# Block sums made beside the second half's input, and a norm between the layers without empty places, in a two-layer trunk

## The chip, the cores and the metric

The kernel runs on one core of one Trainium2 chip. The metric is the device time of one execution in microseconds (us); the median of three runs of the kernel before is 2228.72 us (2227.24 to 2230.06).

## The reference, cut to what matters

Two layers (DEPTH = 2) over x of 1024 positions by 1024 channels, all float32. Per layer, with shift, scale and gate from the conditioning vector:

```python
u = x * (1.0 + scale) + shift
proj = u @ w_in            # a_in, a_gate, b_in, b_gate, q_lat, kv_lat, k_rope, c_gate, merge
# branch A: GLU, causal conv(31), LayerNorm, swish, gate; branch B: short conv, gate
# branch C: latent attention from rms_norm(q_lat), rms_norm(kv_lat), k_rope
m = g_a * y_a + g_b * y_b + g_c * y_c
x = layer_norm(ALPHA * x + gate * (m @ w_o))
```

## The kernel before, in words

**Layout and products.** Everything is stored with channels on the 128 partitions. The 1024 positions are two halves of 512 (T); a tile of u is 128 channels by 512 positions, kept as a pair (high, low) of rounded float32: `split` (L125 to L133) lets ACT round the value (L129) and DVE subtract it for the remainder (L130). Each product block is three matmuls (high·high, high·low, low·high: L186 to L188 in `chunk`, L295 in `pair_jobs`).

**u and its sums.** The eight channel tiles of half h are `state["u", l, h]`. The same tiles are, by parity of the channel tile, the blocks X11 and X12 (first half), X21 and X22 (second half). `pair_jobs` makes two 128-wide outputs for both halves with seven block products instead of eight; its inputs are X11, X12, X22 and the sums S1 to S4 of four tiles each. `s_job` (L493) makes one tile of each sum: it loads the four x tiles again (`affine`, L456, L459), applies scale and shift on ACT (L462), forms S3 = X11 − X21, S1 = X21 + X22, S2 = X22 − S3, S4 = X12 − S2 on DVE (L498, L501, L503, L506) and splits each into its home (`factor`). Temporary tiles have the tag `w`, six buffers in all, which latents, gates and merge tiles use as well; tag `n` has five.

**Start of a layer.** `build` (L1191 on) makes a list of jobs. For each layer it first writes the latents of the first half (`head(l, 0)`: two chunks of kv, three of q, the kv norm and k_rope; 27 jobs, `lat0`), with a side list woven between them: in layer 0 the eight `u_jobs` of the second half (load, affine on ACT, split into X21 or X22), in layer 1 the norm between the layers, `ln_jobs(0, 1)`. Then come the latents of the second half (`lat1`, 24 jobs), with the four `s_job`s woven between them, then the logit pairs (`lgps`, L860), blended with the up-projections (`kps` and others), and the rest.

**The norm between the layers.** `center_jobs` (L740) has a mean (L757), eight centerings with their squares (L762 to L768), `rstd_jobs` (fold of the squares on PE L530, root and Newton step L534 to L539, a row L515, spread on PE L545) and then `apply` for each of eight tiles: multiplication (L1103, DVE), u of the next layer by ACT straight from it (L1107, `through` holds the combined scale and shift), x itself (L1109), its write to HBM from POOL's queue (L1116), and after each odd tile the two splits into X21 and X22 (`add_u`). X21's tiles take the buffers c0 to c3, which held the residual tiles that are written out. The first half of x was normalized before, within layer 0's last part, and its u tiles are made from HBM by `u_jobs(1, 0)`.

**Order.** The place in the job list sets the priority of an instruction; the queue of each engine is then ordered ahead of the run from these priorities and from which operands and buffers are free, so an instruction can stand in its queue before one of an earlier job. `weave(main, side, start, end)` (L66) spreads the side list evenly over the places start to end of the main list. An empty job (`pause`) takes a place and issues nothing. Weights are loaded up to four units ahead (LOOKAHEAD) on SP's queue, as are the x tiles (L459) and the rope tables.

Of the kernel before, what the change touches and what calls it, by code (L numbers as in the profile page):

```python
# [16 lines left out]
P = 128  # L17
T = 512
# [47 lines left out]
def weave(main, side, start, end):  # L66

    out = list(main[:start])
    n, m, k = end - start, len(side), 0
    for i in range(start, end):  # L70
        out.append(main[i])
        upto = (i - start + 1) * m // n
        out += side[k:upto]
        k = upto
    return out + side[k:] + list(main[end:])
# [25 lines left out]
class Trunk:  # L101
# [388 lines left out]
            nc.vector.tensor_tensor(gb[:, 8:16], gb[:, 8:16], a[:, 1], op=ALU.add)  # L490
        return self.state["through"]

    def s_job(self, l, i):  # L493

        nc = self.nc
        tt = nc.vector.tensor_tensor
        x11, x21 = (self.affine(l, h, 2 * i, act=True) for h in range(2))
        tt(x11, x11, x21, op=ALU.subtract)  # L498
        self.factor(l, "S3", x11)
        x22 = self.affine(l, 1, 2 * i + 1, act=True)  # L500
        tt(x21, x21, x22, op=ALU.add)  # L501
        self.factor(l, "S1", x21)
        tt(x22, x22, x11, op=ALU.subtract)  # L503
        self.factor(l, "S2", x22)
        x12 = self.affine(l, 0, 2 * i + 1, act=True)
        tt(x12, x12, x22, op=ALU.subtract)  # L506
        self.factor(l, "S4", x12)
# [229 lines left out]
            return ([], fn)  # L737
        return [step(k) for k in range(31)]

    def center_jobs(self, tiles, n, st, tags, tot=None):  # L740

        nc = self.nc

        def total(_):
            ts = st["ts"] = tiles()
            if tot is not None:
                st["tot"] = tot()
                return
            st["tot"] = self.t2("n", "tot")
            nc.vector.tensor_tensor(st["tot"], ts[0], ts[1], op=ALU.add)  # L750
            for t in ts[2:]:
                nc.vector.tensor_tensor(st["tot"], st["tot"], t, op=ALU.add)

        def mean(_):
            c = st["ts"][0].shape[-1]
            st["ps"] = self.bank("meanps", tags[0])[:, :c]
            nc.tensor.matmul(st["ps"], self.ones, st["tot"], start=True, stop=True)  # L757

        def center(i):
            def fn(_):  # L760
                t = st["ts"][i]
                nc.vector.scalar_tensor_tensor(t, st["ps"], -1.0 / n, t, op0=ALU.mult, op1=ALU.add)  # L762
                sq = self.t2("n", "lsq", t.shape[-1])
                nc.scalar.activation(sq, t, AF.Square)
                if i == 0:
                    st["ss"] = sq
                else:
                    nc.vector.tensor_tensor(st["ss"], st["ss"], sq, op=ALU.add)  # L768
            return ([], fn)
        pause = ([], lambda _: None)  # L770
        fold, spread = self.rstd_jobs(st, n, "ln", tags[1:])
        return [([], total), pause, ([], mean)] + [center(i) for i in range(n // P)] + [pause, pause, fold, pause, pause, pause, spread]

    def lna_jobs(self, l, h):
# [316 lines left out]
        return self.chunk([(self.wo[l, e, :, 0:T], tags[0]), (self.wo[l, e, :, T:2 * T], tags[1])],  # L1091
                          lambda: self.state["m", l, h], post, "ops", "pj", cols, kept)

    def ln_jobs(self, l, h, cols=slice(0, T)):
        nc = self.nc
        st = {}
        n = cols.stop - cols.start

        def apply(e):
            def fn(_):  # L1100
                r = st["ts"][e]
                v = self.vec[l]
                nc.vector.tensor_tensor(r, r, st["r"], op=ALU.mult)  # L1103
                if l < L - 1 and h == 1:
                    t = self.t2("w", "xu")
                    gb = self.through(l)
                    nc.scalar.activation(t, r, AF.Identity, bias=gb[:, 8 + e:9 + e], scale=gb[:, e:e + 1])  # L1107
                    st["t", e] = t
                nc.scalar.activation(r, r, AF.Identity, bias=v[:, V_LB + e:V_LB + e + 1],  # L1109
                                     scale=v[:, V_LG + e:V_LG + e + 1])  # L1110
                if l == L - 1:
                    dst = self.out[e * P:(e + 1) * P, h * T + cols.start:h * T + cols.stop]
                else:
                    dst = self.pd.tile([P, T], F32, name=f"xD{h}{e}")
                    self.state["x", h, e] = dst
                (nc.sync if l == L - 1 else nc.gpsimd).dma_start(dst, r)  # L1116
                if l < L - 1 and h == 1 and e % 2:

                    for k in (e - 1, e):
                        self.add_u(l + 1, h, k, st["t", k])  # L1120
            return ([], fn)
        return self.center_jobs(lambda: [self.state["r", l, h, e][:, cols] for e in range(8)], 1024, st,
                                ("tp", "tp", "av"), lambda: self.state["rt", l, h, cols.start]) \
            + [apply(e) for e in range(8)]

    def end_jobs(self, l, h, cols):
# [64 lines left out]
    def build(self):  # L1191
        self.setup_early()
        jobs, first, adas = [], [], []
        for l in range(L):
# [3 lines left out]
            if l == 0:  # L1198
                lat0, up0 = self.head(l, 0, (("pj", "pj"), ("pj", "sd", "sd")))
                units = [u for us, _ in lat0[:20] for u in us][:10]  # L1200
                for n in range(4):
                    steps = self.ada_jobs(0, n, early=True)
                    for _, fn in steps[:-1]:
                        fn(None)
                    if n == 0:
                        self.nc.sync.dma_start(self.vec[0], self.vecs[0])
                    steps[-1][1](None)
                    if n == 0:
                        self.setup()
                    for k in range(SP[n], SP[n + 1]):  # L1210
                        first.append(self.load_w((units[k], HOMES["first"][k])))
                    self.u_job(0, 0, 2 * n)
                    self.u_job(0, 0, 2 * n + 1)
                tabs = self.table_jobs()
                part0 = weave(lat0, tabs, 2, len(lat0) - 2)
                side0 = self.u_jobs(l, 1)
                adas = [j for n in range(4, 6) for j in self.ada_jobs(0, n)]
            else:
                lat0, up0 = self.head(l, 0)
                part0 = lat0  # L1220
                side0 = self.ln_jobs(l - 1, 1)
            jobs += weave(part0, side0, 0, len(part0))

            lat1, kvn1, ukv1, qn1, uq1 = self.head(l, 1)
            sums = [([], lambda _, l=l, i=i: self.s_job(l, i)) for i in range(4)]
            jobs += weave(lat1, sums, 3, len(lat1) - 2)

            lg = [self.logit_pair(l, n, 2 * i) for n in range(3) for i in range(4)]
            body = blend(lg[0] + lg[1] + lg[2], up0[:-1] + kvn1 + up0[-1:])
# [32 lines left out]
            else:  # L1262

                kept = [{} for _ in range(8)]
                tags = HOMES["wo"]
# [126 lines left out]
```

## Time and profile before

| | |
|---|---|
| median of 3 runs | 2228.72 us |
| the profiled execution | 2231.88 us, its span 2230.0 us |
| mean granted clock of PE | 0.979 |
| busy: PE, DVE, ACT, POOL | 96%, 81%, 51%, 11% of the span |
| HBM read, written | 254.16 MB, 80.54 MB |

The span is what the profiler saw from the first to the last instruction; the execution's own time is 1.9 us longer. A matmul's end is modelled, so busy PE is not PE at its peak; times between starts of matmuls are the better measure. "Granted clock" is the share of full speed that the throttle gave TensorE: its levels are 1.2 and 2.4 GHz. A line of a timeline gives start, duration, engine, source line, operation, out<-in, shape and count; in brackets stands the idle time of the engine before it and what ended it. L129 and L130 are one line for all splits, so they are told apart by their tiles (`u`, `wsplit`, `latn`).

### The profile page before, as it was taken

The numbers are of one execution on the slowest core, as the hardware profiler recorded it, in microseconds if no ns is written. First come the engines' busy times: TensorE is split into PE (matmuls) and PEld (weight loads), VectorE is DVE, ScalarE is ACT, GpSimd is POOL, SyncE is SP. The second block draws the span as 40 slices with busy tenths as digits, with TensorE's granted clock in tenths as the row PEclk, the third lists the DMA queues.
The fourth block names the chain that finished last, engine by engine and source line by source line (L and its number), as shares of the span: only waits on it lengthen the run. The fifth ranks groups of instructions, "written<-read, shape, count | busy, mean of one in ns | idle before, by whom it ended". The sixth has DMA issues, their size and how long they took to land.

```text
span 2230.0 us, 29769 instructions
## 1 busy us (share of the span) xinstructions
PE 2136.2 (96%) x10097; PEld 1730.9 (78%) x10097; DVE 1809.0 (81%) x2910; ACT 1135.0 (51%) x2072; POOL 235.0 (11%) x483
## 2 busy tenths in 40 slices
PE   8889999999999989998997899999999999999996
PEld 7667778888778778877876688888887778888786
DVE  4676899989997678788868769898898967877886
ACT  2764443333344666666448544443434437666843
POOL 4010100000001331111001101000000023221000
PEclk9999999999999999998999999999999999999998
DMA  7566652332222996766535756432222159746542
GB/s 268 177 187 210 162 186 98 104 104 95 76 81 91 229 240 183 198 175 209 189 111 184 204 164 185 148 109 86 90 81 74 61 156 232 213 128 173 167 148 65
DMA packets 185192, 336.68 MB, mean 151 GB/s; under 512 B 22608, under 2 KB 47440, under 8 KB 185040
## 3 DMA queue, kind: packets, MB, share of 16 engines
q1 hardware_dynamic: 124560, 218.50, 31.6%
q0 software_dynamic: 46656, 91.12, 15.6%
q10 hardware_dynamic: 13824, 25.17, 3.1%
q8 instruction: 79, 1.29, 0.2%
q14 instruction: 73, 0.60, 0.1%
HBM read 254.16 MB, written 80.54 MB: 150 GB/s over the span
## 4 chain that ended last, share of the span: by engine, by line
PE 76%; issue 14%; DMA 4%; DVE 3%; ACT 2%; POOL 1%; SPq 0%; POOLq 0%; DVEq 0%; ACTq 0%
PE lgps L295 18%; PE bgps L295 7%; PE xgps L295 7%; PE aps L295 7%; PE cgps L295 4%; PE agps L295 3%; PE yps L186 3%; PE avps L954 3%; PE yps L187 3%; PE yps L188 3%; PE tps L938 3%; PE ops L186 2%; PE ops L187 2%; PE ops L188 2%; PE score L914 2%
## 5 line engine op out<-in xcount | busy, mean ns | idle before, releaser
L295 PE MATMUL lgps<-u,wsplit 128*128 128x512 f32 x2016 | 485.6, 398 | 14.7 <-ACT lgps L260 12.1
L129 ACT CAST wsplit<-wraw 128x512 fp32r<-128x512 f32 (+1 forms) x524 | 318.5, 615 | 294.1 <-PE yps L188 63.9
L295 PEld LDWEIGHTS lgps<-u,wsplit 128*128 128x128 f32 x2016 | 381.0, 189 | 109.9 <-ACT lgps L260 13.9
L130 DVE TENSOR_TENSOR wsplit<-wraw,wsplit 128x512 fp32r<-128x512 f32 (+1 forms) x524 | 353.1, 678 | 72.0 <-ACT wsplit L129 70.7
L736 DVE SCALAR_TENSOR_TENSOR cacc<-abuf,vec,cacc 128x1024 f32<-128x1024 f32 x240 | 306.5, 1277 | 0.6
L295 PE MATMUL xgps<-u,wsplit 128*128 128x512 f32 x672 | 160.4, 397 | 0.0
L295 PE MATMUL bgps<-u,wsplit 128*128 128x512 f32 x672 | 160.0, 397 | 0.0
L295 PE MATMUL aps<-u,wsplit 128*128 128x512 f32 x672 | 158.1, 395 | 0.0
L295 PEld LDWEIGHTS xgps<-u,wsplit 128*128 128x128 f32 x672 | 126.0, 188 | 31.6 <-issue 1.4
L295 PEld LDWEIGHTS bgps<-u,wsplit 128*128 128x128 f32 x672 | 126.0, 188 | 31.5 <-issue 1.4
L295 PEld LDWEIGHTS aps<-u,wsplit 128*128 128x128 f32 x672 | 126.3, 188 | 30.5
L130 DVE TENSOR_TENSOR pt<-tps,pt 128x512 fp32r<-128x512 f32 (+1 forms) x160 | 98.9, 631 | 26.8 <-ACT pt L129 25.3
L919 DVE TENSOR_REDUCE nm<-score 128x1 f32<-128x384 f32 (+7 forms) x128 | 95.7, 750 | 27.5 <-PE score L917 26.5
L186 PE MATMUL ops<-m,wsplit 128*128 128x512 f32 (+1 forms) x320 | 116.0, 364 | 0.6 <-ACT m L129 0.6
L921 ACT ACTIVATE prob<-score,nm 128x384 f32<-128x384 f32 (+7 forms) x128 | 94.3, 739 | 43.8 <-DVE nm L919 23.4
L186 PE MATMUL yps<-y,wsplit 128*128 128x512 f32 x256 | 111.6, 436 | 4.8 <-ACT y L132 4.2
L954 PE MATMUL avps<-pt,Vh 128*128 128x256 f32 x640 | 110.9, 297 | 3.2 <-ACT pt L129 2.1
L187 PE MATMUL ops<-m,wsplit 128*128 128x512 f32 (+1 forms) x320 | 112.3, 351 | 0.6 <-DVE m L130 0.6
L188 PE MATMUL ops<-m,wsplit 128*128 128x512 f32 (+1 forms) x320 | 112.1, 351 | 0.0
L129 ACT CAST pt<-tps 128x512 fp32r<-128x512 f32 (+1 forms) x160 | 84.0, 540 | 42.7 <-PE tps L938 40.1
L187 PE MATMUL yps<-y,wsplit 128*128 128x512 f32 x256 | 104.0, 406 | 0.2 <-DVE y L133 0.2
L129 ACT CAST wsplit<-wt 128x512 fp32r<-128x512 f32 x112 | 69.5, 620 | 68.0 <-DVE wt L220 47.8
(322 smaller groups left out, 4265.4 us busy)
## 6 DMA issues: line engine op xcount, KB each, us to landing
wraw<-in_win SPq DMA_DIRECT2D x264, 256.0 KB, 2.7
wraw<-in_wout SPq DMA_DIRECT2D x96, 256.0 KB, 3.0
mt<-tD SPq DMA_DIRECT2D x96, 256.0 KB, 4.3
adaraw<-in_wada SPq DMA_DIRECT2D x64, 256.0 KB, 3.5
wraw<-in_wo SPq DMA_DIRECT2D x64, 256.0 KB, 3.2
tD<-mt ACTq DMA_DIRECT2D x48, 256.0 KB, 2.1
Kh<-knD POOLq DMA_DIRECT2D x48, 256.0 KB, 4.6
Vh<-vD POOLq DMA_DIRECT2D x48, 256.0 KB, 5.2
```

Source lines behind the costliest of these rows:

```text
L129: nc.scalar.copy(dst[:, 0], src)
L130: nc.vector.tensor_tensor(dst[:, 1], src, dst[:, 0].bitcast(F32), op=ALU.subtract)
L186: mm(ps, w[:, 0, c], x[k][:, 0, cols], start=k == 0, stop=False)
L187: mm(ps, w[:, 0, c], x[k][:, 1, cols], start=False, stop=False)
L188: mm(ps, w[:, 1, c], x[k][:, 0, cols], start=False, stop=k == n - 1)
L295: mm(ps, w[:, a, c], x[:, e], start=n < 2 and k == 0 and i == 0, stop=k == 3 and i == 2, skip_group_check=True)
L736: nc.vector.scalar_tensor_tensor(acc, a[:, k:k + S], w, acc, op0=ALU.mult, op1=ALU.add)
L914: mm(o, q[0:96, 0, qc], k[0:96, 0, :w], start=True, stop=False)
L919: nc.vector.tensor_reduce(nm[:, 0:1], sp[:, :nk], axis=AX.X, op=ALU.max, negate=True)
L921: nc.scalar.activation(p[:, :nk], sp[:, :nk], AF.Exp, bias=nm[:, 0:1], accum_out=nm[:, 1:2])
L938: nc.tensor.transpose(tp[:, c:c + P], st["p", hd, 2 * half + b][:, (2 * kp + k) * P:(2 * kp + k + 1) * P], self.ident)
L954: mm(av[:, half * 256:(half + 1) * 256], v[:, 2 * kp + k], pt[:, w, (1 - k) * 256:(2 - k) * 256], start=kp == 0 and k == 0 and w == 0, sto ...
```

## The change

`s_job` becomes `su_job`. It is handed the two finished tiles of u of the second half, splits them into X21 and X22 and goes on with the sums of the same four tiles, so that it loads and scales only the two tiles of the first half. In layer 0 four such jobs take the place of the eight `u_jobs`, in layer 1 `apply` calls one after each odd tile. The sums woven into `lat1` go; `lat1` stands alone. In the norm between the layers (`tight`) four of six empty places go (the one after `total`, both before `fold`, one of the three behind it): `total, mean, center x8, fold, pause, pause, spread` instead of `total, pause, mean, center x8, pause, pause, fold, pause, pause, pause, spread`.

```diff
--- before.py
+++ after.py
@@ -490,14 +490,14 @@
             nc.vector.tensor_tensor(gb[:, 8:16], gb[:, 8:16], a[:, 1], op=ALU.add)
         return self.state["through"]
 
-    def s_job(self, l, i):
-
-        nc = self.nc
-        tt = nc.vector.tensor_tensor
-        x11, x21 = (self.affine(l, h, 2 * i, act=True) for h in range(2))
+    def su_job(self, l, i, x21, x22):
+
+        tt = self.nc.vector.tensor_tensor
+        self.add_u(l, 1, 2 * i, x21)
+        self.add_u(l, 1, 2 * i + 1, x22)
+        x11 = self.affine(l, 0, 2 * i, act=True)
         tt(x11, x11, x21, op=ALU.subtract)
         self.factor(l, "S3", x11)
-        x22 = self.affine(l, 1, 2 * i + 1, act=True)
         tt(x21, x21, x22, op=ALU.add)
         self.factor(l, "S1", x21)
         tt(x22, x22, x11, op=ALU.subtract)
@@ -737,7 +737,7 @@
             return ([], fn)
         return [step(k) for k in range(31)]
 
-    def center_jobs(self, tiles, n, st, tags, tot=None):
+    def center_jobs(self, tiles, n, st, tags, tot=None, tight=False):
 
         nc = self.nc
 
@@ -769,6 +769,8 @@
             return ([], fn)
         pause = ([], lambda _: None)
         fold, spread = self.rstd_jobs(st, n, "ln", tags[1:])
+        if tight:
+            return [([], total), ([], mean)] + [center(i) for i in range(n // P)] + [fold, pause, pause, spread]
         return [([], total), pause, ([], mean)] + [center(i) for i in range(n // P)] + [pause, pause, fold, pause, pause, pause, spread]
 
     def lna_jobs(self, l, h):
@@ -1091,7 +1093,7 @@
         return self.chunk([(self.wo[l, e, :, 0:T], tags[0]), (self.wo[l, e, :, T:2 * T], tags[1])],
                           lambda: self.state["m", l, h], post, "ops", "pj", cols, kept)
 
-    def ln_jobs(self, l, h, cols=slice(0, T)):
+    def ln_jobs(self, l, h, cols=slice(0, T), tight=False):
         nc = self.nc
         st = {}
         n = cols.stop - cols.start
@@ -1116,11 +1118,10 @@
                 (nc.sync if l == L - 1 else nc.gpsimd).dma_start(dst, r)
                 if l < L - 1 and h == 1 and e % 2:
 
-                    for k in (e - 1, e):
-                        self.add_u(l + 1, h, k, st["t", k])
+                    self.su_job(l + 1, e // 2, st["t", e - 1], st["t", e])
             return ([], fn)
         return self.center_jobs(lambda: [self.state["r", l, h, e][:, cols] for e in range(8)], 1024, st,
-                                ("tp", "tp", "av"), lambda: self.state["rt", l, h, cols.start]) \
+                                ("tp", "tp", "av"), lambda: self.state["rt", l, h, cols.start], tight) \
             + [apply(e) for e in range(8)]
 
     def end_jobs(self, l, h, cols):
@@ -1213,17 +1214,17 @@
                     self.u_job(0, 0, 2 * n + 1)
                 tabs = self.table_jobs()
                 part0 = weave(lat0, tabs, 2, len(lat0) - 2)
-                side0 = self.u_jobs(l, 1)
+                side0 = [([], lambda _, i=i: self.su_job(0, i, *(self.affine(0, 1, 2 * i + e, act=True) for e in range(2))))
+                         for i in range(4)]
                 adas = [j for n in range(4, 6) for j in self.ada_jobs(0, n)]
             else:
                 lat0, up0 = self.head(l, 0)
                 part0 = lat0
-                side0 = self.ln_jobs(l - 1, 1)
+                side0 = self.ln_jobs(l - 1, 1, tight=True)
             jobs += weave(part0, side0, 0, len(part0))
 
             lat1, kvn1, ukv1, qn1, uq1 = self.head(l, 1)
-            sums = [([], lambda _, l=l, i=i: self.s_job(l, i)) for i in range(4)]
-            jobs += weave(lat1, sums, 3, len(lat1) - 2)
+            jobs += lat1
 
             lg = [self.logit_pair(l, n, 2 * i) for n in range(3) for i in range(4)]
             body = blend(lg[0] + lg[1] + lg[2], up0[:-1] + kvn1 + up0[-1:])
```

## Rows read from the trace of the kernel before

**Rows 1.** The page, its span and the busy time of each engine.

```profile
span 2230.0 us, 29769 instructions
PE 2136.2 (96%) x10097; PEld 1730.9 (78%) x10097; DVE 1809.0 (81%) x2910; ACT 1135.0 (51%) x2072; POOL 235.0 (11%) x483
```

**Rows 2.** Timeline of PE: matmuls behind its longest waits around both layers' starts.

```profile
98.05 0.77 PE L186 MATMUL latps<-u,wsplit 128*128 128x512 f32 x1 [4.10 <-DVE kra L599]
...
131.94 2.93 PE L295 MATMUL lgps<-u,wsplit 128*128 128x512 f32 x6 [5.25 <-ACT lgps L260]
...
1183.18 0.80 PE L186 MATMUL latps<-u,wsplit 128*128 128x512 f32 x1 [7.39 <-ACT u L129]
...
1225.91 0.50 PE L307 MATMUL kps<-latn,wsplit 128*128 128x512 f32 x1 [3.99 <-ACT sq L560]
...
1233.29 2.92 PE L295 MATMUL lgps<-u,wsplit 128*128 128x512 f32 x6 [4.55 <-ACT lgps L260]
```

**Rows 3.** Windows of all engines, around the first latents of layer 0 and of layer 1.

```profile
core 0: us, PE busy (x) PEld busy (x) DVE busy (x) ACT busy (x) POOL busy (x), PEclk, DMA share, GB/s
64.00:98.00 34.00, 28.13 (x127) 20.71 (x127) 25.02 (x48) 28.12 (x50) 2.75 (x5) 0.98 0.56 177
98.00:136.00 38.00, 32.71 (x132) 25.18 (x133) 34.72 (x61) 29.73 (x52) 2.15 (x4) 0.86 0.58 192
1175.00:1198.00 23.00, 15.61 (x61) 11.19 (x60) 17.63 (x32) 18.77 (x31) 4.85 (x9) 0.78 0.39 142
1198.00:1237.00 39.00, 30.45 (x132) 22.98 (x131) 34.44 (x60) 32.73 (x57) 3.23 (x6) 0.87 0.62 200
```

**Rows 4.** Timeline of ACT: the two copies L260 and what stood before each.

```profile
130.79 0.62 ACT L129 CAST u<-xu 128x512 fp32r<-128x512 f32 x1
131.31 0.58 ACT L260 COPY lgps<-lgps 128x512 f32<-128x512 f32 x1
...
1232.13 0.62 ACT L129 CAST u<-xu 128x512 fp32r<-128x512 f32 x1
1232.65 0.58 ACT L260 COPY lgps<-lgps 128x512 f32<-128x512 f32 x1
```

**Rows 5.** Timeline of PE, DVE, ACT: the norm before layer 1, to the last X2 tile.

```profile
1163.98 0.42 PE L530 MATMUL qv<-lsq,ones 128*32 128x128 f32 x8
...
1174.70 0.39 PE L545 MATMUL rstd<-rsrow,onesr 128*128 128x512 f32 x1
...
1175.63 4.26 DVE L1103 TENSOR_TENSOR r<-r,rstd 128x512 f32<-128x512 f32 x7
...
1182.53 1.12 ACT L129 CAST u<-xu 128x512 fp32r<-128x512 f32 x2
...
1195.14 0.62 ACT L129 CAST u<-xu 128x512 fp32r<-128x512 f32 x1 [1.53 <-DMA xD<-r]
```

**Rows 6.** Timeline of ACT: several of one kind in a row.

```profile
1208.35 1.65 ACT L129 CAST u<-xu 128x512 fp32r<-128x512 f32 x3
...
1212.66 2.24 ACT L462 ACTIVATE xu<-xu,ada 128x512 f32<-128x512 f32 x3
```

**Rows 7.** Timeline of DVE: the first subtraction of the first and last job of sums.

```profile
1206.55 0.69 DVE L498 TENSOR_TENSOR xu<-xu 128x512 f32<-128x512 f32 x1 [2.23 <-ACT xu L462]
...
1230.16 0.68 DVE L498 TENSOR_TENSOR xu<-xu 128x512 f32<-128x512 f32 x1
```

**Rows 8.** Waits of SP's queue, 60 to 140 us: in total, times, longest.

```profile
SPq L459 <- DVE u L130: 11.8, 8, 4.5
```

**Rows 9.** Timeline of PE: matmuls at low and at full clock, behind the wait at 98.

```profile
103.30 0.62 PE L186 MATMUL latps<-u,wsplit 128*128 128x512 f32 x1
103.73 0.43 PE L187 MATMUL latps<-u,wsplit 128*128 128x512 f32 x1
103.99 0.39 PE L188 MATMUL latps<-u,wsplit 128*128 128x512 f32 x1
104.22 0.39 PE L186 MATMUL latps<-u,wsplit 128*128 128x512 f32 x1
```

## The prediction

> **What bounds the kernel now.** I read the page first: PE is busy for 2136.2 of 2230.0 us [rows 1]. So at most some 94 us of waiting can be won in the whole span, and only where PE waits in the stretches that the change touches.
>
> The second view is PE's own timeline over the two starts (layer 0 up to 140 us, layer 1 from 1140 us). Five waits of about 4 us or more stand there, 25.3 us together [rows 2]; the reader should look at what each ended on. 7.39 us in layer 1 is the first latent product of the second half, waiting for the first X2 tile. 4.10 us in layer 0 is the same product waiting for a PSUM bank that k_rope's DVE work (L599) had not given back. The other three stand behind the latents: two `lgps` products (5.25 and 4.55 us) end on the copy L260, one `kps` product (3.99 us) on the square L560. L260 and L560 are short ACT instructions that were merely late.
>
> The third view, the windows, says why they were late. While the jobs of sums run (98 to 136 and 1198 to 1237 us) DVE is busy 34.7 of 38 and 34.4 of 39 us, ACT 29.7 of 38 and 32.7 of 39 [rows 3]. In the stretches just before (64 to 98, 1175 to 1198) DVE has 9.0 and 5.4 us to spare, ACT 5.9 and 4.2. ACT's timeline shows both late copies directly behind a cast of a `u` tile [rows 4]; at that place it belongs to a sum. So PE waits for two vector engines that are filled with sums, and just before that they have some room.
>
> The fourth view follows the norm between the layers: squares folded on PE at 1163.98, spread at 1174.70, first multiplication of `apply` at 1175.63, first X21 cast at 1182.53, last X2 cast at 1195.14 [rows 5]. DVE runs seven L1103 in a row, though the code writes them pair by pair: the place in the job list is a priority, not the place in the queue.
>
> **The change, part by part.** *Loads and affines removed.* Per layer the sums no longer load the second half's eight x tiles again: 8 DMAs of 256 KB and 8 affines L462. The loads are worth nothing by themselves: the DMA share in these stretches is 0.39 to 0.62 [rows 3]. The affines cost ACT (2.24 us for three, so 0.75) 6.0 us per layer [rows 6], already left out of the next price.
>
> *Sums moved in front of the second half's latents.* One pair's sums now cost ACT two affines (1.5) and four casts (1.65 us for three, so 0.55 each, 2.2): 3.7 us [rows 6]; DVE eight instructions at 4.26/7 = 0.61 [rows 5]: 4.9 us. They have priority over the next pair's X2 tiles, and PE needs all eight X2 tiles for the first latent chunk. Three pairs' sums lie before the last X2 tile, so it comes later by at most 3 × 3.7 = 11.1 us if ACT sets the pace. It is less where loads and affines of the first half, which wait for nothing of the second, run in ACT's spare time: with all six early, 3 × 2.2 = 6.6 us. It is more if a pair's sums take the pace they have today: 1206.55 to 1230.16 for three jobs is 7.9 us each [rows 7], less two affines 6.4, and 3 × 6.4 = 19.2 us. I take 9.6: one pair's affines early (1.5 us off), the rest in line, because ACT's spare time holds about that and the price of single instructions is nearer to a queue that is never empty. DVE, with 4.9 us a pair against 9.0 and 5.4 to spare, follows within these ends.
>
> *SP and POOL.* On SP the loads of the first half's x (eight a layer) now stand ahead of weights. A load whose buffer is still in use blocks SP: 11.8 us in eight times today [rows 8]. Weights are asked for four units ahead, which covers a few us; with that cover gone it belongs to the upper end, 19.2. POOL's writes of x keep number and order. The first sum of a pair (S1) gains a wait: it overwrites x21, so it follows X21's split, whose cast waits for the write of the residual out of the same buffer (1.53 us before the last cast [rows 5]); behind it on ACT stand only casts of the same pair, counted above.
>
> *What the late sums gave back.* After the latents nothing of the sums is left in front of L260 and L560, so these waits go: 3.99 + 4.55 us in layer 1, 5.25 in layer 0 [rows 2]. Each left a low clock. Behind the 4.10 us wait the matmuls start 0.43 us apart, back to 0.23 from 103.99 on [rows 9]: 13 matmuls took 103.73 − 98.05 = 5.7 us where 13 × 0.23 = 3.0 would do, 2.7 us lost at the low level (1.2 GHz). Behind the two `lgps` waits six matmuls took 2.92 us instead of 1.4 [rows 2], so 1.5 to 2.7 us; I take 2. Behind 3.99 the first matmul ran 0.50 us, near full, so 0 to 2.7: I take 1. Gain: layer 1 3.99 + 1 + 4.55 + 2 = 11.5, layer 0 5.25 + 2 = 7.3 us. Next in line then are the weights' splits, which PE reaches one unit at a time.
>
> In layer 0 the 4.10 us wait with its 2.7 lies inside the latents, where PE will now wait for X2 tiles anyway: 6.8 us of the delay is absorbed there.
>
> *The norm without pauses.* Four of six empty places go and 22 jobs instead of 26 are spread over 27: the mean comes after the third instead of the fourth product job, the fold after the 14th instead of the 15th, the spread after the 18th instead of the 19th. A place is six matmuls of 0.23, 1.4 us. An empty place waits for nothing, so bounds are nothing (the DVE chain, not the place, rules) and half the 10.7 us between fold and spread [rows 5], 5.3; a loss only if PE reached the spread before its row was there, one place, 1.4. I take a gain of one place, 1.4.
>
> *Sum.* Layer 1: −1.4 + 9.6 − 11.5 = −3.3. Layer 0: 9.6 − 6.8 − 7.3 = −4.5. Together −7.8 us. The profiled execution took 2231.9 us around its span of 2230.0; it would take 2224.1. It stands 3.2 us above the median of 2228.7, which becomes 2220.9: 2221.
>
> **The rivals.** *More: the vector engines' spare time takes the sums.* Where all affines of the first half run early, the delay is 6.6 us: layer 0 is 6.6 − 6.6 − 7.3 = −7.3, layer 1 with the norm's best −5.3 + 6.6 − 11.5 = −10.2; together −17.5, 2211. For it: DVE's 9.0 and 5.4 us to spare. Against it: ACT has little more than 4 us just before.
>
> *Slower: the six `w` buffers pace the pairs.* A pair now holds four of them (x21, x22, x11, x12) until S4, and in layer 0 the two kv latents hold two more up to their norm, so one pair at a time gets through. Then today's pace of sums holds, 19.2 us: layer 1 −1.4 + 19.2 − 11.5 = +6.3, layer 0 19.2 − 6.8 − 7.3 = +5.1; +11.4, 2240. For it: 11.8 us of SP's waits on exactly that release [rows 8]. Against it: the chunks' drains shared those buffers and both engines then. It decides from where both layers' delays exceed 11.5 + 14.1 + 1.4 = 27.0, so 13.5 us each, 4.5 a pair.
>
> *No change: the clock takes it back.* X2 pairs come 12.6/3 = 4.2 us apart today [rows 5]; with 3.2 us of sums each it is 7.4, and for each pair PE has 12 matmuls on two banks, 2.8 us at 0.23: waits of over 4 us, as long as those that left a low level above. Then each layer runs a low stretch more, 2.7 each [rows 9]: −7.8 + 5.4 = −2.4, 2226. The Trainium skill, "TensorE: Matmul & The Clock Gate", section on HAM oscillation, speaks against the change in the same way: groups of matmuls shorter than the wait between them begin at the low clock each time. By that rule the sum would be −2.4 instead of −7.8; the trace agrees so far as every wait above 4 us is followed by 0.43 us matmuls, but while the next pair is still missing a slow group costs nothing, and only the last one counts.
>
> **How the numbers follow.** A measurement of this kernel tells about 0.2%, 4.5 us, from no change: faster is below 2224.3, slower above 2233.2. Chances: forecast 0.42 (its own range 2214 to 2227), more 0.20 (2200 to 2215), clock 0.16 (2223 to 2230), slower 0.22 (2231 to 2248). Faster: three quarters of the first, all of the second, a fifth of the third: 0.55. Same: a quarter of the first, most of the third, a tenth of the fourth: 0.25. Slower 0.20. The range 2207 to 2239 leaves out about a third of "more" and half of "slower", under 0.2.
>
> **What would show it.** Right: 16 L462 fewer (eight per layer); the last X2 cast of layer 1 near 1204 instead of 1195; PE's waits on L260 and L560 behind the latents gone, and new, shorter ones on `u` casts between the latent products; DVE fuller in 1175 to 1198. The norm is right if fold and spread come 1 to 2 us earlier. Wrong: waits on L260 as long as before (then it was not the sums), pairs more than 8.5 us apart (slower), or 0.43 us matmuls after each pair up to the last latent (clock).

## The result and the profile after

The change made the kernel slower: 2243.28 us (median of 7 runs, 2235.21 to 2248.02) against 2228.94 us of the kernel before on the same chip, ratio 1.0063, 95% interval 1.0048 to 1.0077, so 10.7 to 17.2 us. The prediction was 2221 us, faster. The profiled execution of after took 2248.02 us, its span is 2246.1.

The page of after, span and busy times:

```profile
span 2246.1 us, 29725 instructions
PE 2140.1 (95%) x10097; PEld 1729.3 (77%) x10097; DVE 1811.3 (81%) x2910; ACT 1124.9 (50%) x2056; POOL 234.8 (10%) x483
```

Against [rows 1] 16 ACT instructions are gone, as the change says. PE is busy 3.9 us longer for the same 10097 matmuls and idle some 12 us longer. Lines of the listing from L771 to L1118 stand two further down in after.

To see where, I cut the start of each layer at three marks that every kernel has. In layer 0 the first is **S**, a matmul of the first half's latents that ends a wait of 0.49 us on a split weight, so that what happened ahead of it drops out; then come the last latent product of the second half and the first product `aps` (the first of the pair products behind the latents). In layer 1 they are the last `prime` (its start), the last latent product and the last `aps`. From before, the timeline of PE (first line) and groups of a tile on PE, which give count, min/median/max ns, and first to last start:

```profile
64.38 0.50 PE L188 MATMUL latps<-u,wsplit 128*128 128x512 f32 x1 [0.49 <-DVE wsplit L130]
L188 PE MATMUL latps<-u,wsplit x59: 387/396/632, 59.9 to 117.8; 128*128 128x512 f32 x59
L295 PE MATMUL aps<-u,wsplit x672: 393/394/399, 217.4 to 1595.8; 128*128 128x512 f32 x168
L203 PE MATMUL prime<-onesr x6: 392/564/793, 1.3 to 1141.3; 128*128 128x512 f32 x6
L188 PE MATMUL latps<-u,wsplit x80: 390/394/796, 1142.0 to 1215.0; 128*128 128x512 f32 x80
```

The same of after:

```profile
62.41 0.50 PE L188 MATMUL latps<-u,wsplit 128*128 128x512 f32 x1 [0.49 <-DVE wsplit L130]
L188 PE MATMUL latps<-u,wsplit x57: 387/397/628, 60.2 to 134.5; 128*128 128x512 f32 x57
L295 PE MATMUL aps<-u,wsplit x672: 393/394/398, 226.5 to 1609.1; 128*128 128x512 f32 x168
L203 PE MATMUL prime<-onesr x6: 392/562/796, 1.3 to 1152.6; 128*128 128x512 f32 x6
L188 PE MATMUL latps<-u,wsplit x80: 391/396/628, 1153.3 to 1237.8; 128*128 128x512 f32 x80
```

**A** (S to the last latent product, layer 0) went from 53.4 to 72.1 us; **B** (from there to the first `aps`) from 99.6 to 92.0; **C** (`prime` to the last latent product, layer 1) from 73.7 to 85.2; **D** (from there to the last `aps`) from 380.8 to 371.3. So both layers lose up to the last latent and get back behind it: layer 1 most of it, layer 0 two fifths. The rest of the run has the same jobs in both, but it is not equally long in every profile: from the first `aps` to `prime` it took 919.5 to 926.1 us over all kernels of this document. So what single profiles add up to A to D is not the difference of the medians to the microsecond.

PE's waits in after, timeline of PE, in answer to [rows 2]:

```profile
83.38 0.73 PE L186 MATMUL latps<-u,wsplit 128*128 128x512 f32 x2 [2.40 <-ACT u L129]
...
97.58 0.80 PE L186 MATMUL latps<-u,wsplit 128*128 128x512 f32 x1 [7.74 <-ACT u L129]
104.91 0.73 PE L186 MATMUL latps<-u,wsplit 128*128 128x512 f32 x2 [1.56 <-ACT u L129]
...
115.19 0.79 PE L186 MATMUL latps<-u,wsplit 128*128 128x512 f32 x1 [4.50 <-ACT sq L560]
...
147.07 6.47 PE L295 MATMUL lgps<-u,wsplit 128*128 128x512 f32 x20 [1.87 <-ACT lgps L260]
...
1194.54 0.79 PE L186 MATMUL latps<-u,wsplit 128*128 128x512 f32 x1 [7.41 <-ACT u L129]
1199.85 0.80 PE L186 MATMUL latps<-u,wsplit 128*128 128x512 f32 x1 [2.00 <-ACT sq L560]
1211.40 0.50 PE L186 MATMUL latps<-u,wsplit 128*128 128x512 f32 x1 [4.12 <-ACT u L129]
...
1250.31 4.93 PE L295 MATMUL lgps<-u,wsplit 128*128 128x512 f32 x20 [1.87 <-ACT lgps L260]
```

What went as foreseen: the L260 waits fell from 5.25 and 4.55 to 1.87 each, and the `kps` wait on L560 is gone. What was not: the 4.10 us of [rows 2] in layer 0 has a successor of 4.50 us on a square, ahead of the same product, and the waits for X2 tiles came on top of it.

Windows of all engines in after: the stretches of [rows 3], then A, then C:

```profile
core 0: us, PE busy (x) PEld busy (x) DVE busy (x) ACT busy (x) POOL busy (x), PEclk, DMA share, GB/s
64.00:98.00 34.00, 21.42 (x91) 14.86 (x89) 24.66 (x43) 25.29 (x43) 1.67 (x3) 0.87 0.56 177
98.00:136.00 38.00, 31.44 (x118) 22.57 (x118) 30.88 (x58) 23.54 (x44) 2.84 (x6) 0.80 0.37 119
62.00:134.50 72.50, 52.96 (x206) 37.57 (x207) 55.60 (x100) 49.41 (x86) 4.37 (x8) 0.84 0.46 147
1152.60:1237.80 85.20, 70.37 (x294) 52.05 (x293) 73.71 (x133) 59.60 (x103) 8.62 (x16) 0.90 0.40 131
```

The first row is the surprise. More work was put into 64 to 98 us, yet DVE and ACT are busy *less* there than before (24.66 and 25.29 against 25.02 and 28.12), with over 8 us to spare on each. Up to 98 us they were not too full; they waited. Waits of SP's queue in after, 60 to 140 us (total, times, longest):

```profile
SPq L459 <- DVE u L130: 11.7, 6, 8.1
SPq L459 <- DMA latq<-lat: 6.7, 2, 4.7
SPq L459 <- DVE xu L503: 3.6, 2, 2.1
```

The total of the first line is that of [rows 8], but one wait is 8.1 us long instead of 4.5 at most: loads of x stand at SP's head until a `w` buffer is free. The Trainium skill, "DMA: Bandwidth & Descriptors", section "Anatomy of one DMA", says that a wait for a semaphore is taken by the issuing sequencer and not by the DMA engines. These rows agree: all three waits stand in SP's queue.

### The profile page after: what moved, and what is told of

Read it like the earlier page. It is cut to its first block, busy times and chain, and to the rows that moved or that the text cites. A ratio compares the mean times of both kernels' runs of the same rounds, so it can differ in the third digit from the quotient of the medians.

```text
span 2246.1 us, 29725 instructions
## 1 busy us (share of the span) xinstructions
PE 2140.1 (95%) x10097; PEld 1729.3 (77%) x10097; DVE 1811.3 (81%) x2910; ACT 1124.9 (50%) x2056; POOL 234.8 (10%) x483
## 4 chain that ended last, share of the span: by engine, by line
PE 79%; issue 9%; DMA 5%; DVE 4%; ACT 2%; POOL 0%; SPq 0%; POOLq 0%; DVEq 0%; ACTq 0%
PE lgps L295 20%; PE bgps L295 7%; PE xgps L295 7%; PE aps L295 7%; PE cgps L295 3%; PE agps L295 3%; PE yps L186 3%; PE yps L187 3%; PE yps L188 3%; PE avps L956 3%; PE tps L940 3%; PE ops L186 2%; PE ops L188 2%; PE ops L187 2%; PE score L916 1%
## 5 line engine op out<-in xcount | busy, mean ns | idle before, releaser
L295 PEld LDWEIGHTS lgps<-u,wsplit 128*128 128x128 f32 x2016 | 379.4, 188 | 100.1 <-ACT lgps L260 4.6
L188 PE MATMUL ops<-m,wsplit 128*128 128x512 f32 (+1 forms) x320 | 112.0, 350 | 0.0
L186 PE MATMUL latps<-u,wsplit 128*128 128x512 f32 x160 | 71.4, 457 | 38.8 <-ACT u L129 32.0
```

The lines of the kernel that those rows point to most:

```text
L186: mm(ps, w[:, 0, c], x[k][:, 0, cols], start=k == 0, stop=False)
L188: mm(ps, w[:, 1, c], x[k][:, 0, cols], start=False, stop=k == n - 1)
L295: mm(ps, w[:, a, c], x[:, e], start=n < 2 and k == 0 and i == 0, stop=k == 3 and i == 2, skip_group_check=True)
```

## The experiments

Fourteen kernels, each timed in five rounds beside the kernel before (medians of it 2229.9 to 2230.6 us; every ratio is to its own). A to D are from the one profiled execution of each. In the kernels that hold tiles, L459 and L462 stand three lines further down (L462, L465). Kernels with the same code in a stretch agree within 2.3 us in A, 3.2 in B, 0.3 in C and 2.8 in D.

| kernel | median us | ratio, 95% | A | B | C | D |
|---|---|---|---|---|---|---|
| before | | | 53.4 | 99.6 | 73.7 | 380.8 |
| the change | 2243.28 | 1.0063 (1.0048, 1.0077) | 72.1 | 92.0 | 85.2 | 371.3 |
| layer 0 alone | 2242.54 | 1.0049 (1.0031, 1.0066) | 72.5 | 91.0 | 73.7 | 383.0 |
| layer 1 alone | 2229.63 | 1.0000 (0.9988, 1.0011) | 52.0 | 98.4 | 85.0 | 372.1 |
| tiles held | 2240.33 | 1.0048 (1.0030, 1.0065) | 65.4 | 91.1 | 90.1 | 371.3 |
| no sum ahead | 2227.66 | 0.9983 (0.9971, 0.9994) | 50.2 | 96.7 | 75.1 | 383.2 |
| X2 first | 2234.59 | 1.0020 (1.0008, 1.0032) | 66.1 | 91.4 | 83.3 | 373.4 |
| norm alone | 2229.55 | 0.9992 (0.9979, 1.0005) | 52.9 | 96.4 | 73.8 | 382.1 |
| no sum ahead, layer 0 | 2227.88 | 0.9984 (0.9970, 0.9998) | 50.1 | 96.7 | 73.6 | 382.8 |
| without the norm | 2244.03 | 1.0059 (1.0040, 1.0078) | 72.0 | 91.3 | 85.3 | 371.3 |
| held, layer 0 | 2238.53 | 1.0042 (1.0027, 1.0057) | 67.7 | 92.6 | 73.7 | 383.6 |
| one ahead | 2219.73 | 0.9953 (0.9935, 0.9971) | 52.5 | 94.6 | 75.3 | 377.4 |
| two ahead | 2218.92 | 0.9952 (0.9939, 0.9965) | 55.4 | 92.4 | 76.0 | 373.0 |
| one ahead, tiles loaded again | 2226.52 | 0.9985 (0.9973, 0.9998) | 54.6 | 95.3 | 75.7 | 379.4 |
| three ahead | 2228.36 | 1.0001 (0.9990, 1.0011) | 62.5 | 90.6 | 82.5 | 371.9 |
| two between | 2228.68 | 0.9999 (0.9989, 1.0009) | 60.9 | 94.1 | 79.1 | 373.9 |

**Which layer.** `su_job` in layer 0 only (layer 1 as before, no `tight`), and the other way round:

```diff
-            sums = [([], lambda _, l=l, i=i: self.s_job(l, i)) for i in range(4)]
+            sums = [([], lambda _, l=l, i=i: self.s_job(l, i)) for i in range(4)] if l else []
```

> The change in layer 0 alone (layer 1 and its norm as before). Theory B (buffers: a pair that holds four of the six w buffers makes the next pair's loads wait) and theory E (engines: the sums' instructions stand in front of the X2 tiles on ACT and DVE) both expect that layer 0 carries most of the loss, since the first aps product came 9.1 us later there: 2238 us, 2234 to 2242. If layer 1 carries it, 2229.

> The change in layer 1 alone, with the norm without empty places (layer 0 as before). Both theories: the rest of the loss, between 2 and 5 us by the marks of the two traces: 2229 to 2235, 2232 likeliest.

Layer 0 alone is the change's loss (2242.54 us, 0.5 above the range I gave), layer 1 alone is worth nothing: 11.3 us lost in C, 10.4 got back in D, against the means of the kernels with layer 1 unchanged (73.7 and 382.5).

**Buffers.** The change, with x21 and x22 of a pair in the home that S4's pair takes later, so that a pair holds two `w` buffers instead of four; then the same in layer 0 alone.

```diff
+    def held(self, i):
+        return self.pa.tile([P, 2, T], F32, tag=HOMES["S4"][i], name="xh")
...
+                    xh = self.held(i)
+                    self.su_job(0, i, *(self.affine(0, 1, 2 * i + e, act=True, x=xh[:, e]) for e in range(2)))
```

> The change in full, but x21 and x22 of a pair lie in the buffer that S4 of this pair takes later, so a pair holds two w buffers instead of four. Theory B: the loads of the first half no longer wait, the last X2 cast of layer 0 comes before 97 us (104 in the change, 91 before), and the time falls to 2231 or less. Theory E: the last X2 cast stays at 100 us or later in layer 0 and 8 us or more later than before in layer 1, and the time stays at 2238 or more.

> The change in layer 0 alone (layer 1 as in the kernel before), with x21 and x22 in S4's home so that a pair holds two w buffers instead of four. Theory (two causes in layer 0: the w buffers cost some 7 us, the sums' work in front of the latents the rest): from 62 us to the last product of the second half's latents about 65 us, where the change in layer 0 alone took 72.4 and the kernel before 55.8; layer 1 as before; 2233 to 2238, 2235 likeliest. Rival (the buffers are all of it): 55 to 58 us there and 2226 to 2231. Rival (the buffers are nothing, a gap of single profiles): 72 us and 2240 to 2244.

With the full change neither theory holds: PE's last wait for an X2 cast in layer 0 ends at 93.62 us, as theory B had it, but the time of 2240.33 is theory E's. A falls from 72.2 (mean of three) to 65.4 and 67.7: 4.4 to 6.8 us of A go with the buffers. The whole time does not show it: the median with layer 0 alone goes from 2242.5 to 2238.5, above the range I gave, but the intervals of the two ratios overlap. In layer 1 the step does harm: C rises from 85.2 to 90.1. The X2 tiles are not the reason, for PE's last wait for one ends 60.8 us behind `prime` there, against 67.2 in the change; what lies behind it is longer, 29.4 against 18.0 us, at a granted clock of 0.82 against 1.00. So the buffers were not all; why layer 1 is worse off without their limit is not shown. Of SP's waits for x loads with layer 0 alone, same columns as above, those on `u` have shrunk from 11.7 to 5.0 us, while those on the write of `latq` grew from 6.7 to 10.7. PE's last wait for an X2 cast (second fence, timeline of PE) ends 32.3 us behind S (62.17), where in the change it ends after 42.5:

```profile
SPq L462 <- DMA latq<-lat: 10.7, 2, 6.5
SPq L462 <- DVE u L130: 5.0, 2, 4.1
```

```profile
94.44 0.50 PE L186 MATMUL latps<-u,wsplit 128*128 128x512 f32 x1 [1.29 <-ACT u L129]
```

**What is left out is worth little, and where the sums stand.** The next kernels keep x21 and x22 in S4's home as well and leave out the second loads and affines, but put the sums elsewhere: at their old places between the latents (none ahead), or behind all X2 splits and ahead of the latents.

```diff
-            jobs += weave(lat1, sums, 3, len(lat1) - 2)
+            jobs += sums + lat1
```

> Kernel before with the removed work alone taken out: x21 and x22 are kept (in the buffer of S4) and the sums use them, but stand where they stood before, between the latents of the second half. 8 loads and 8 affines a layer less, X2 tiles not behind any sum. Both theories: the last X2 casts as before (91 and 1195 us), ACT 6 us less filled a layer while the sums run, the waits on L260 and L560 shorter: 2218 to 2226, 2222 likeliest. If the removed work is worth nothing: 2229. If the waits in front of the sums were the loads' own buffers: 2215 or less.

> Second half's tiles kept in layer 0 alone, sums at their old places; layer 1 is the kernel before. Theory (the removed loads and affines are worth about 5 us in layer 0 and nothing in layer 1): 2220 to 2228, 2224 likeliest. Rival (the gain of the run with both layers was spread over both, or chance of that run): 2226 to 2231.

> x21 and x22 are kept in S4's home, so loads and affines of the second half are gone as in the change, but the jobs of sums stand behind all eight X2 splits and ahead of the second half's latents, in both layers. Theory E (sums that come ahead of the X2 tiles in the list delay them): X2 casts as early as with the sums at their old places (last one near 84 us in layer 0, some 54 us after layer 1's prime), and what is left are waits of 2 to 5 us a layer on squares and copies behind the latents; 2226 to 2234, 2229 likeliest. Rival (the sums cost the same wherever they stand ahead of the latents): 2236 to 2242, 2239 likeliest.

With none ahead, 0.9983 of before: that is what the removed loads and affines are worth, together with the two `w` buffers that a pair no longer holds, 1.3 to 6.5 us, and layer 0 alone has all of it. With all four behind the X2 tiles the gain is more than gone, 1.0020, just past the range of either theory. X2's last affine is 21.8 us behind S in both, so the place ahead of the X2 tiles can't be what makes A 66.1 instead of 50.2 there. It is the amount of sums ahead of the latents. Windows over A, no sum ahead, then (next fence) all four, there also the part from 93 to 112 us:

```profile
62.00:111.20 49.20, 45.60 (x204) 34.69 (x203) 41.19 (x77) 41.11 (x72) 4.37 (x8) 0.97 0.53 169
```

```profile
62.00:127.70 65.70, 49.54 (x206) 35.90 (x205) 54.37 (x99) 48.34 (x85) 4.37 (x8) 0.84 0.44 139
93.00:112.00 19.00, 6.41 (x12) 3.27 (x13) 18.83 (x32) 14.05 (x25) 1.62 (x3) 0.54 0.25 81
```

DVE has 13.2 us more to do and the stretch is 16.5 us longer. The average of DVE is 0.84 and 0.83, but it hides where DVE is full: from 93 to 112 us it is busy 18.83 of 19.00 us, and PE 6.41. Most of PE's idle time there is one wait, on the square of a latent (timeline of PE, all four behind X2; L569 is L560 of before):

```profile
103.48 0.79 PE L186 MATMUL latps<-u,wsplit 128*128 128x512 f32 x1 [8.17 <-ACT sq L569]
```

Ahead of that square and its copy stand three casts and an affine of sums on ACT, and the first of them waited 1.52 us for DVE. So the drains of the latents (copy, square, norm), which give PE its banks back, come behind the sums. PE's own work is 45.6 of 49.2 us with none ahead, so there is little slack to hide that in.

**The norm.** The kernel before with `tight` alone, and the change without it.

```diff
-                side0 = self.ln_jobs(l - 1, 1, tight=True)
+                side0 = self.ln_jobs(l - 1, 1, tight=False)
```

> The kernel before with the norm without empty places alone. Theory (the DVE chain and ACT set the restart of PE behind the norm, not the places in the list; PE's restart came 42.5 us after the prime in both kernels): within 0.2% of before, 2225 to 2233, 2229 likeliest. Rival, the prediction's step: one place earlier, 1.4 us faster, up to 5.3. Rival of a loss (the fold's and the spread's matmuls now wait in PE's queue for their rows): 2 to 6 us slower.

> The change with the norm's empty places back. Theory (the norm's part is worth nothing, all of the loss is the sums' place): 2240 to 2246, 2243 likeliest. Rival, the prediction's step: 1.4 to 5.3 us slower than the change, 2244 to 2249. Rival of a harmful norm: 2236 to 2240.

Worth nothing in either: C is 73.8 against 73.7, and 85.2 against 85.3. Timeline of PE in the kernel with `tight` alone:

```profile
1159.04 0.43 PE L530 MATMUL qv<-lsq,ones 128*32 128x128 f32 x8
...
1170.00 0.39 PE L545 MATMUL rstd<-rsrow,onesr 128*128 128x512 f32 x1
1177.98 0.79 PE L186 MATMUL latps<-u,wsplit 128*128 128x512 f32 x1 [7.59 <-ACT u L129]
```

From its `prime` at 1135.9 the fold comes after 23.1 us, the spread after 34.1, the restart after 42.1; before they were 22.7, 33.4 and 41.9 ([rows 5], [rows 2], `prime` at 1141.3). Not one of the three moved forward, so the places do not set them; PE's restart ends on an ACT cast. What sets the fold and the spread was not tested.

**How many sums ahead.** One, two or three of the four behind the X2 splits and ahead of the latents, the others between the latents as before:

```diff
-            jobs += weave(lat1, sums, 3, len(lat1) - 2)
+            jobs += sums[:2] + weave(lat1, sums[2:], 3, len(lat1) - 2)
```

> The deferred version (second half's tiles kept in both layers, sums woven between the second half's latents) with one of the four sums of each layer put ahead of the latents, behind all X2 splits. Theory (PE has next to no spare time up to the last latent, so each sum put ahead of the latents costs its share): with none ahead the stretch from 62 us to the last latent product took 49.2 us, with all four ahead 65.7, so 52 to 55 with one; the end 2228 to 2231. Rival (the vector engines have room for one, only the later ones cost): 49 to 51 and 2225 to 2228.5.

> As the version with one sum ahead of the latents, but two of four, in both layers. Theory (beside the X2 tiles and the latents' drains the vector engines have room for about one sum; each further one costs its share): from 62 us to layer 0's last latent product 49.2 us with none, 51.4 with one, 65.7 with four, so (65.7 - 51.4)/3 = 4.8 more, 56 us; layer 1 from the prime to the last latent product 75.1, 75.3, 83.3, so 78; what stands behind them gets 1 to 2 us shorter in each layer; 2221 to 2228, 2224 likeliest. Rival (room for two): 51 to 53 us in layer 0, 75 to 76 in layer 1, 2213 to 2220.

> Three of a layer's four sums ahead of the second half's latents, behind all X2 splits, tiles kept. With two ahead nothing was lost, with four the gain was gone. Theory (the loss is of each sum past the second): halfway, 60 us from 62 us to layer 0's last latent product (54.4 with two, 65.7 with four), about 79.5 us in layer 1 (76.0 and 83.3), the end 2222 to 2230, 2226 likeliest. Rival (the loss comes with the fourth sum alone): 55 to 57 us, 76 to 77 us, 2216 to 2222.

> The kernel before with nothing changed but that one of a layer's four sums stands ahead of the second half's latents, behind all X2 splits; tiles are loaded and scaled again as before. Theory (the place of one sum is most of what the last version but one won, the kept tiles the lesser part): the stretch behind the latents of layer 1 some 5 us shorter (380.8 before), 2221 to 2226, 2223 likeliest. Rival (the sum pays only with kept tiles, since its four loads wait for w buffers and its four affines fill ACT): 2228 to 2234.

I missed the first two; three ahead came out inside the range of its theory. One ahead costs 2.3 us in A and gets back 2.1 in B and 5.8 in D; two cost 5.2 and 0.9 and get back 4.3 and 10.2, nearly all that four give. The third adds 7.1 us to A and 6.5 to C and gets back 1.8 and 1.1. So the gain is had with two and the price is in the third and fourth. Two ahead is the fastest kernel of the study, 2218.92 us (2216.74 to 2222.72), 7.8 to 13.6 us faster than before, and one ahead can't be told from it. Its page and marks:

```profile
span 2215.6 us, 29701 instructions
PE 2129.2 (96%) x10097; PEld 1723.5 (78%) x10097; DVE 1806.0 (82%) x2910; ACT 1124.2 (51%) x2056; POOL 235.4 (11%) x483
```

```profile
61.01 0.50 PE L188 MATMUL latps<-u,wsplit 128*128 128x512 f32 x1 [0.49 <-DVE wsplit L130]
L188 PE MATMUL latps<-u,wsplit x56: 387/394/796, 61.0 to 116.4; 128*128 128x512 f32 x56
L295 PE MATMUL aps<-u,wsplit x672: 393/394/398, 208.8 to 1579.8; 128*128 128x512 f32 x168
L203 PE MATMUL prime<-onesr x6: 389/566/793, 1.3 to 1130.8; 128*128 128x512 f32 x6
L188 PE MATMUL latps<-u,wsplit x80: 388/398/628, 1131.5 to 1206.8; 128*128 128x512 f32 x80
```

One ahead with the tiles loaded again, as before, took 0.9985, between the two ranges on record: the place and the kept tiles pay best together. A likely reason, not tested, is that a sum that has to load and scale four tiles instead of two brings that work ahead of the latents too.

**Place against amount.** Two sums again, but each directly behind its own pair's X2 splits, ahead of the other X2 tiles, as the change has it:

```diff
+        if h and kt in (1, 3):
+            self.s_job(l, kt // 2)
```

> As the version with two sums ahead of the latents, but each of the two stands directly behind its own pair's X2 splits, so ahead of the other X2 tiles, as in the change. Theory P (the place ahead of X2 tiles costs, since PE needs all eight before its first chunk ends): PE waits for u casts longer, last X2 cast several us later in both layers, 2222 to 2230. Theory A (only the amount of sums ahead of the latents' end counts): 2216 to 2221, as with two behind the X2 tiles.

The place costs as well: 2228.68 instead of 2218.92, with intervals apart; A 60.9 instead of 55.4 (from a profiled execution of 2233.09 us, slower than the median). Timeline of ACT, the affines of X2 (first to last start), two between, with S at 65.27, then two behind, with S at 61.01:

```profile
L465 ACT ACTIVATE xh<-xh,ada x8: 801/817/827, 67.1 to 92.4; 128x512 f32<-128x512 f32 x8
```

```profile
L465 ACT ACTIVATE xh<-xh,ada x8: 799/812/821, 62.8 to 82.7; 128x512 f32<-128x512 f32 x8
```

The last one starts 27.1 us behind S instead of 21.7, so 2.7 us later per sum ahead of it. With four sums the place makes no further difference in layer 0 (A 66.1 behind, 65.4 and 67.7 between): the amount already sets the end there. In layer 1 C is 83.3 and 90.1.

## Why the prediction was wrong

By its own steps, with the unchanged layers' means (A 52.8, B 98.1, C 73.7, D 382.5) against those of the kernels that have the change's layer (A 72.2, B 91.4, C 85.2, D 371.6):

| | predicted | measured |
|---|---|---|
| layer 0, up to the last latent (A): 9.6 − 6.8 | +2.8 | +19.4 |
| layer 0, behind it (B) | −7.3 | −6.7 |
| layer 1, norm and up to the last latent (C): −1.4 + 9.6 | +8.2 | +11.5 |
| layer 1, behind it (D) | −11.5 | −10.9 |
| sum | −7.8 | +13.3 |

- *Loads and affines removed*: right that they are worth little: 1.3 to 6.5 us, two freed buffers included, when the sums stay where they were.
- *What the late sums gave back*: right in kind, and the size agrees to 0.6 us in both layers. That is closer than kernels of the same code agree (3.2 us in B, 2.8 in D), so it is partly luck, and the waits on L260 did not go but fell to 1.87 us. Two sums would have given nearly all of it.
- *Sums moved in front of the latents* is the step that failed, in layer 0 above all, and in two of its terms. **The delay of the last X2 tile** was taken as 9.6 us from ends of 6.6 and 19.2. It is 15.4 in layer 0: the last X2 cast ends at 104.85 in after, 42.4 us behind S, against 27.0 before (the fences below, timeline of ACT). In layer 1 it starts 66.5 us behind `prime`, against 53.8 ([rows 5] and 1141.3): 12.7. The price of a sum by itself was near: 2.7 us measured with the tiles in another home, 3.2 taken. What I put aside were the buffers: with x21 and x22 out of the `w` buffers PE has the last X2 tile of layer 0 10.2 us earlier (32.3 and 42.5 us behind S, above).
- **The 6.8 us "absorbed"** were not, and this term was off by more. From the end of the last X2 cast to the last latent product it is 26.4 us before and 29.7 in after, 3.3 longer where the sum had 6.8 less. The prediction took the wait of 4.10 us for that of the second half's first latent product. It is not (third fence, before: a line of PE's timeline, then groups of `latps`): 16 of that half's 40 products L188, its two kv chunks, run ahead of it, and they use the last X2 tile at 91.47 us. So the wait lies behind the last X2 tile, and a later tile shifts what is ahead of the wait as well. Ahead of the same product PE then waited 4.50 us on L560 (last fence, after: again 24 products L188 follow): on the squares of those two kv chunks, which stood on ACT behind casts of sums (second fence, the lines from 111.74 on).
- So the path was wrong too: the prediction let the moved sums cost no more than the delay of the last X2 tile. With the sums behind all X2 tiles that delay is gone, and A is still 66.1, 13.3 us above the mean of 52.8. With the tiles held, in layer 0 alone, it is 5.2 us by PE's waits, and A is 14.9 above.

Before:

```profile
90.81 0.61 ACT L129 CAST u<-xu 128x512 fp32r<-128x512 f32 x1
```

After:

```profile
103.73 1.12 ACT L129 CAST u<-xu 128x512 fp32r<-128x512 f32 x2
...
111.74 1.15 ACT L129 CAST u<-xu 128x512 fp32r<-128x512 f32 x2
...
113.30 0.62 ACT L129 CAST u<-xu 128x512 fp32r<-128x512 f32 x1
...
114.54 1.08 ACT L560 ACTIVATE sq<-latps 128x512 f32<-128x512 f32 x2
...
1219.12 0.62 ACT L129 CAST u<-xu 128x512 fp32r<-128x512 f32 x1 [0.86 <-DMA xD<-r]
```

Before, PE's use of the last X2 tile, and the products ahead of the wait of 4.10 us and behind it:

```profile
91.47 0.50 PE L186 MATMUL latps<-u,wsplit 128*128 128x512 f32 x1 [0.40 <-ACT u L129]
L188 PE MATMUL latps<-u,wsplit x16: 390/397/398, 79.9 to 93.6; 128*128 128x512 f32 x16
L188 PE MATMUL latps<-u,wsplit x24: 391/398/632, 99.0 to 117.8; 128*128 128x512 f32 x24
```

After, behind the wait of 4.50 us:

```profile
L188 PE MATMUL latps<-u,wsplit x24: 391/396/628, 116.2 to 134.5; 128*128 128x512 f32 x24
```

- The bottom of it is the reading of "room": 9.0 and 5.9 us idle on DVE and ACT in 64 to 98 us [rows 3]. The prediction set the 4.9 us of DVE work of one pair against all of DVE's idle time; the three pairs that it put ahead of the last X2 tile are 14.7. And the idle time was not where the sums came to stand: with the tiles held in layer 0 alone DVE was busy 24.97 of 25.00 us from 75 to 100 us; with none ahead it was busy already 16.88 of 18.20 us from 93 us to the last latent product.
- *The norm without pauses*: 1.4 us predicted, none measured. The norm's events came 0.2 to 0.7 us later, not earlier.

The rivals. *Slower: the `w` buffers* had the time nearest (2240) and its mechanism is there, but it was less than half of layer 0's loss. Its condition, delays of over 27.0 us in the two layers together, was just met (15.4 + 12.7 = 28.1); by its own sum that made +1.1 us, and most of the rest lies in the wait that was not absorbed. *The clock takes it back* is at most a part: with layer 1 alone changed, layer 0's stretch stood so (windows over A):

```profile
62.00:114.40 52.40, 46.89 (x207) 35.40 (x208) 41.48 (x77) 43.50 (x76) 4.37 (x8) 0.97 0.60 194
```

Against 52.96 us for 206 matmuls in after that is 6.1 us of slower matmuls, at a granted clock of 0.84 instead of 0.97 (means over the two levels, 1.2 and 2.4 GHz); the other 14 us of the longer stretch are waits. The Trainium skill, "TensorE: Matmul & The Clock Gate", section on HAM oscillation, tells of a kernel whose groups of matmuls, each shorter than the wait behind it, begin at the low clock every time. The trace went that way. I had put it at one low stretch, 2.7 us a layer, and held that slow groups cost nothing while the next pair is missing; how much of the 6.1 us counts is not shown, since a slow group that ends before a wait takes nothing from the end. *More* is excluded for all four sums: DVE's spare time did not take them.

## What to carry to other kernels

When work of a side engine is moved ahead of a stretch in which the bounding engine has little slack, move as much of it as that stretch takes and no more: here half the sums gave nearly all the gain, and the other half cost it. Read the side engine's room where the bounding engine would wait, not from an average: DVE's 0.83 over A was 0.99 in the 19 us in which PE mostly stood still. Then test with one part, two parts, three. Ask of every wait that the plan counts as covered whether it stands ahead of the delay or behind it. And count buffers along the new path: a tile kept "because it is there anyway" holds a place in the pool until its last reader, and here the next load waited at the head of its queue.

## What the runs showed that was not expected

- With the tiles held, the stretch up to layer 0's last latent grew with DVE's work: 41.19 us in 49.2, 43.20 in 51.4, 45.86 in 54.4, 49.46 in 61.4, 54.37 in 65.7 (none, one, two, three, four sums ahead), 0.81 to 0.84 of it. It is no rule: two between has 48.60 in 64.2 (0.76), the change with its buffers 55.60 in 72.5 (0.77), layer 1 alone 41.48 in 52.4 (0.79).
- ACT's part and DVE's part were not told apart: PE waits on ACT's squares, these stand behind casts that wait for DVE, and no run moved work from one of the two to another engine, or set the drains ahead of the sums in the list.
- A shortage of buffers went with a shorter stretch once: with six `w` buffers for everything, C was 85.2; with x21 and x22 outside of them 90.1.
- Why the third sum costs so much more than the second (7.1 against 2.9 us in A) was not settled; the runs show the step, not what sets its place.
